# Last squares summed by TensorE, a fuller scan end, and later modulation in a two-block network

## The chip, the cores and the metric

The kernel runs on one core of one Trainium2 chip. The metric is device time of one execution in microseconds (us), as the median of three runs. TensorE is called PE in the rows, VectorE DVE, ScalarE ACT, GpSimd POOL and SyncE, which issues most transfers, SP.

## The reference, cut to what matters

Sequence 512, width 1024, batch 1, all in float32. A first block of two layers is followed by a second block of one even and one odd mixer and a final norm.

```python
def first_block(x, mem, positions, ...):
    h = x
    for l in range(2):
        hn = rms_norm(h, norm_mix_pre[l])
        proj = hn @ w_in[l]                     # split in 12 parts
        y_attn = dilated_attention_mixer(...)   # 256 wide
        y_conv = short_conv_mixer(...)          # 256 wide
        y_gdn = gated_deltanet_mixer(...)       # 512 wide; a scan over 8 chunks of 64
                                                # positions, then o = rms_norm(o, w) * gate
        mix = concatenate([y_attn, y_conv, y_gdn]) @ w_out[l]
        h = h + rms_norm(mix, norm_mix_post[l])
        hn = rms_norm(h, norm_xattn_pre[l])
        xa = memory_cross_attention(hn, rms_norm(mem, norm_mem[l]), w_xq[l], w_xkv[l], w_xo[l])
        h = h + rms_norm(xa, norm_xattn_post[l])
        hn = rms_norm(h, norm_ffn_pre[l])
        h = h + rms_norm(swiglu_ffn(hn, w_gate_up[l], w_down[l]), norm_ffn_post[l])
    return h

def second_block(x, c, ctx, c_ctx, mod_w, mod_b, norm_g, ...):
    for i in range(2):
        sh_l, sc_l, g_l = split(silu(c) @ mod_w[i] + mod_b[i], 3)      # the modulation
        sh_c, sc_c, g_c = split(silu(c_ctx) @ mod_w[i] + mod_b[i], 3)
        h_lat = rms_norm_2(x, norm_g[i]) * (1 + sc_l) + sh_l
        h_ctx = rms_norm_2(ctx, norm_g[i]) * (1 + sc_c) + sh_c
        y, y_ctx = (even_mixer if i == 0 else odd_mixer)(h_lat, h_ctx, ...)
        x = x + g_l * y                          # the odd mixer holds a 31-tap depthwise
        ctx = ctx + g_c * y_ctx                  # convolution beside its attention
    return rms_norm_2(x, final_g)
```

## The kernel before, in words

*Layout.* Everything is feature-major: the residual stream `hT` is 8 chunks of 128 features by 512 positions. A matrix product runs in three products of rounded float32 (`mm3`, lines 293 to 295): weight and input are each split in a high part (`wh`, `xh`) and a residual (`wl`, `xl`), and high x high, high x low and low x high are summed in PSUM. One output tile of 128 x 512 is 8 chunks x 3 = 24 matmuls. A weight tile arrives by DMA from SP's queue (`wr`, 3 buffers), is rounded on ACT (`wh`, line 266) and its residual taken on DVE (`wl`, line 267), 4 buffers each. PSUM has three kinds of tile, two of each: `g` and `b` of one bank, `s` of two.

*Statistics.* The RMS norms need a sum over features, that is over partitions. ACT squares each chunk (line 392), DVE adds the squares into `acc` (line 393), and TensorE multiplies `acc` with a matrix of ones in full float32 (line 378, in `rsqrt_of`); ACT makes R, the reciprocal root, from the sum with Ln and Exp. `residual_stat` (line 404) does so for each output chunk that TensorE leaves in PSUM, after copying it to `om`. `residual` (line 409) then scales `om` by R, adds it to `hT`, splits the new chunk into `xh` and `xl` for the next product, which is begun with each chunk (`begin`, `advance`), and `prestat` (line 429) takes the statistics of the new `hT` for the next norm. That R is applied when the product's tiles are evicted (line 454, `fg`). Such ends stand at mix_post, x_post and f_post of each layer.

*What sets the order.* Each engine runs its instructions in the order in which a scheduler set them at build time; priorities follow the order of the code. Where a chain leaves TensorE without work, the code interleaves other work by generators: `self.fill` is a list of them, `pump(n)` takes n steps from the first, `drain` takes all. The memory's and the context's projections, the gates and the short convolution are such fills. Rates say how many steps come with one piece of the main work: RATES[l] in the feed-forward part of layer l (layer 1's fill is the context stream, `ctx_stream`), CR in odd attention, where the fill is the 31-tap convolution on DVE (`conv31`, line 1777) and what surrounds it, spread over 32 items of attention.

*The scan's end.* `gdn_scan` (line 822) runs eight chunks in sequence. The last one's output goes to `O` (L855 is its last product), then `gdn_norm` (line 880) four times: ACT squares, DVE scales `O`, TensorE transposes it (line 888), DVE multiplies it into `om`. `mix_out` had begun tiles 0 and 1 of w_out with input chunks 0 to 3, which come from attention and convolution; behind the norms chunks 4 to 7 are split and `advance`d.

*The first block's end.* `residual` of f_post1 leaves the new `hT`; `colstat` (line 1355) squares its 8 chunks, adds 7 of them on DVE, sums on TensorE; `modnorm` (line 1335) makes `xh` and `xl` chunk by chunk with R and the modulation, and TensorE starts the even mixer's first product (`ev_in`). The context stream is pumped around it.

*The modulation* (`mod_dot`, line 1311) is 96 dot products of 1024 elements on DVE with weights from `mw`, a fill of layer 0's feed-forward part. They may not be issued before a named instruction: `last`, the last split of x_post0's residual.

Of the kernel before, what the change touches and what calls it, by code (L numbers as in the profile page):

```python
# [12 lines left out]
AF = mybir.ActivationFunctionType  # L13
# [4 lines left out]
D = 1024  # L18
S = 512
CTX = 256  # L20
MEM = 256
KC = D // 128
HID = 2816
HC = HID // 128
# [5 lines left out]
TS, TB = 2, 2  # L30
WP, XP = 1, 2
ER, OR = 1, (1.6, 2.1, 2.1, 1.7)
CR = 1.5
XOP = (0, 1)
RATES = (0.7, 1.1)
WR, WH, WL = 3, 4, 4
HA, HB, HD = 0, 0, 0
MP = (0, 0)
# [172 lines left out]
class Net:  # L211
# [128 lines left out]
    def begin(self, aps, extra=0):  # L340
# [7 lines left out]
        for i, ap in enumerate(aps):  # L348
            wh, wl = self.weight(ap)
            self.begun.append(((ap.tensor.name, ap.offset), wh, wl, ps[i]))  # L350

    def advance(self):
        c = self.nbegun
        self.nbegun += 1
        for _, wh, wl, ps in self.begun:
            self.mm3(ps, wh[:, c], wl[:, c], self.xh[:, c], self.xl[:, c], c == 0, c == KC - 1)


    def pump(self, n=1):
# [15 lines left out]
    def rsqrt_of(self, ss, out, scale, epscol, n=512, lhs=None):  # L375
        nc = self.nc
        ps = self.bps()[:, :n]
        nc.tensor.matmul(ps, self.ones if lhs is None else lhs, ss, start=True, stop=True)  # L378
        bias = 0.0 if epscol is None else self.epst[:, epscol:epscol + 1]
        nc.scalar.activation(out, ps, AF.Ln, bias=bias, scale=scale)  # L380
        nc.scalar.activation(out, out, AF.Exp, scale=-0.5)
        return ps

    def sumsq(self, acc, src, first, t=None):

        nc = self.nc
        if first:
            nc.scalar.activation(acc, src, AF.Square)
        else:
            if t is None:  # L390
                t = self.tmp("sq")[:, :acc.shape[-1]]
            nc.scalar.activation(t, src, AF.Square)  # L392
            nc.vector.tensor_add(acc, acc, t)  # L393

    def split(self, h, l, src, w=None):

# [5 lines left out]


    def residual_stat(self, c, ps, acc):
        nc = self.nc
        nc.scalar.copy(self.om[:, c], ps)
        self.sumsq(acc, ps, c == 0)

    def residual(self, acc, post, pre=None, R=None, scale=1.0 / D, epscol=0, chunk=2, aeps=0, keep=False):
        nc = self.nc  # L410
        Rp = self.R
        self.pump(2)
        with self.hp(HA):
            self.rsqrt_of(acc, Rp, 1.0 / D, aeps)
        self.pump(3)
        for c in range(KC):
            self.pump(chunk)
            t = self.tmp("rt")
            with self.hp(HB):
                nc.vector.scalar_tensor_tensor(t, self.om[:, c], self.sm(post, c), Rp, ALU.mult, ALU.mult)  # L420
                nc.vector.tensor_add(self.hT[:, c], self.hT[:, c], t)
                if pre is not None:
                    self.last = self.split(self.xh[:, c], self.xl[:, c], self.hT[:, c], self.sm(pre, c))
            if pre is not None:
                self.advance()
        if pre is not None:
            self.prestat(R, scale, epscol, keep)

    def prestat(self, R, scale=1.0 / D, epscol=0, keep=False):
        nc = self.nc  # L430
        acc = self.tmp("acc2", bufs=1)
        for c in range(KC):
            self.sumsq(acc, self.hT[:, c], c == 0)
        ps = self.rsqrt_of(acc, R, scale, epscol)
        if keep:

            self.zacc = self.tmp("acc", bufs=1)
            nc.scalar.activation(self.zacc, ps, AF.Identity, bias=self.epst[:, 3:4], scale=8.0 * EPS / D)
# [17 lines left out]
    def out_proj(self, w, pump=0):  # L456
        acc = self.tmp("acc", bufs=1)
        for c in range(KC):
            ps = self.gemm(w[c], (self.xh, self.xl))
            self.residual_stat(c, ps, acc)  # L460
            self.pump(pump)
        return acc

    def silu(self, out, x, t):

# [39 lines left out]
    def first(self, dbg=None):  # L505
# [5 lines left out]
        for l in range(2):  # L511
            self.mark(f"mix{l}")
            self.mixer(l)
            if dbg and dbg(self, f"mix{l}"): return
            self.mark(f"xattn{l}")
            self.xattn(l)
            if l == 0:
                with tc.tile_pool(name="md", bufs=1) as p:
                    self.mod_start(p)
                    csb = self.mod_rows(p)  # L520
                    dots = [self.mod_dot(i, p, csb, 0, 24) for i in range(2)]
                    acc = self.xo_ffn(l, dbg, 1, dots + [self.mod_end(0), self.mod_end(1)])
                    self.drain()
                    self.begin([w[1][c] for c in range(2)], 2)
                    self.residual(acc, "f_post0", "mix_pre1", self.R, chunk=1, aeps=None)
                if dbg and dbg(self, f"h3_{l}"): return
            else:
                self.ctxp = self.ctx.enter_context(tc.tile_pool(name="keep", bufs=1))
                self.Vc = self.ctxp.tile([128, 2, 2, 128], F32, name="vc")
                self.kd = [[self.dr.tile([128, CTX], F32, name=f"kd{i}{u}") for u in "hl"] for i in range(6)]  # L530
                self.dv = self.ctxp.tile([128, 2, 512], F32, name="dvc")
                with tc.tile_pool(name="ctx", bufs=1) as p:
                    self.fill = [self.ctx_stream(p)]
                    acc = self.xo_ffn(l, dbg, 1)
                    self.residual(acc, "f_post1", chunk=1, aeps=None)
                    if dbg and dbg(self, f"h3_{l}"): return
                    self.mark("ctxend")
                    R = self.colstat(self.hT, S, self.R)
                    self.pump(2)
                    self.begin([a["ev_in"][c] for c in (4, 0, 5)])  # L540
                    for _ in self.modnorm(0, 0, self.hT, self.xh, self.xl, S, R):
                        self.advance()
                        self.pump()
                    self.drain()
# [277 lines left out]
    def gdn_scan(self, l, p, heads):  # L822
# [3 lines left out]
        for c in range(8):  # L826
# [38 lines left out]
            if c == 7:  # L865
                while len(self.fill) > 3:
                    self.pump()
                for i in range(4):
                    self.gdn_norm(l, O, i, p)
        self.drain()  # L870
        self.mark(f"gdnend{l}")
        for h in range(4):
            self.split(self.xh[:, 4 + h], self.xl[:, 4 + h], self.om[:, 4 + h])
            self.advance()

    def gdn_norm(self, l, O, i, p):

# [330 lines left out]
    def ffn(self, l, rate):  # L1208
# [13 lines left out]
        w = max(PARTS[l])  # L1222
        ends = np.cumsum(PARTS[l]).tolist()
        parts = list(zip([0] + ends, ends))
        def down(ti, yh, yl):
            lo, hi = parts[ti]
            for c in range(KC):
                ps = self.gemm(a["w_down"][l][c][:, lo:hi], (yh, yl), k=hi - lo)
# [1 line left out]
                    nc.scalar.copy(self.om[:, c], ps)  # L1230
                else:
                    nc.vector.tensor_add(self.om[:, c], self.om[:, c], ps)  # L1232
                    if hi == HC:
                        self.sumsq(acc, self.om[:, c], False)
                step()

        with tc.tile_pool(name=f"ff{l}", bufs=2) as p:
# [73 lines left out]
    def mod_dot(self, i, p, csb, n0, n1):  # L1311

        nc, a = self.nc, self.a
        last = self.last[1].ins
        for n in range(n0, n1):
            raw = self.tmp("mw", (128, 2, 512), pool=p, bufs=2).rearrange("p a b -> p (a b)")
            nc.sync.dma_start(raw, a[f"mod_t{i}"][n - 4 * MP[i]])
# [531 lines left out]
```

## Time and profile before

| | |
|---|---|
| median of 3 runs | 2509.55 us (2506.88 to 2512.07) |
| profiled execution | 2508.96 us |
| its span | 2507.2 us |
| mean granted clock of TensorE | 0.986 |
| TensorE busy | 2409.2 us, 96% |
| VectorE busy | 1755.7 us, 70% |
| ScalarE busy | 1272.1 us, 51% |
| DMA | 263.30 MB, mean 105 GB/s |

All rows are of one profiled execution; times in them count from the start of its span. The busy time of TensorE is modelled from the ends of pipelined matmuls. A timeline row is: start, duration, engine, line, operation, output<-inputs, count, and in brackets how long the engine sat idle ahead of it and for what. A window row is: stretch, its length, then busy time and number of instructions of PE, weight loads (PEld), DVE, ACT and POOL, the granted clock (1.00 is full), the DMA engines' mean share and GB/s.

### The profile page before, as it was taken

What the parts mean: (1) busy time and instruction counts of PE and PEld (TensorE: products, weight loads), DVE (VectorE), ACT (ScalarE), POOL (GpSimd) and SP (SyncE); (2) the same over time, 40 slices, a digit from 0 to 9 for tenths busy, and PEclk for the clock granted to TensorE, in tenths of its full rate; (3) what the DMA queues carried; (4) which work ended last, traced back from release to release, by engine and by line L of the source; (5) the groups of instructions that cost most, each with busy time, mean ns of one, the idle gap of its engine ahead of it and who ended that gap; (6) DMA issues with size and microseconds to landing.
All of it is one profiled execution on the core that took longest, in us unless ns stands there. A gap on an engine that the chain in (4) does not pass through costs nothing.

```text
span 2507.2 us, 34818 instructions
## 1 busy us (share of the span) xinstructions
PE 2409.2 (96%) x13036; PEld 1960.1 (78%) x13036; DVE 1755.7 (70%) x3164; ACT 1272.1 (51%) x2371; POOL 22.6 (1%) x57
## 2 busy tenths in 40 slices
PE   8999899989999989998999999999998999999998
PEld 6678688768888766786887678888876888878787
DVE  7887675499984578876755755556566666669975
ACT  5754454444333447544545644445344666545584
POOL 0000000000000000000000000000000000000000
PEclk9999999999999999999999999999999999999999
DMA  5133133237753321331332233233335421333422
GB/s 180 51 86 77 51 118 126 93 115 238 214 174 109 97 83 51 86 77 51 125 120 78 83 97 97 93 100 127 118 116 155 119 64 56 115 101 99 115 77 68
DMA packets 96025, 263.30 MB, mean 105 GB/s; under 512 B 16232, under 2 KB 32232, under 8 KB 94704
## 3 DMA queue, kind: packets, MB, share of 16 engines
q1 hardware_dynamic: 92592, 257.72, 33.8%
q0 software_dynamic: 704, 2.17, 0.5%
q10 hardware_dynamic: 2560, 1.18, 0.3%
q8 instruction: 103, 1.69, 0.3%
q14 instruction: 66, 0.54, 0.1%
HBM read 240.83 MB, written 4.46 MB: 98 GB/s over the span
## 4 chain that ended last, share of the span: by engine, by line
PE 84%; DVE 9%; ACT 3%; DMA 2%; issue 2%; ACTq 0%; DVEq 0%; SPq 0%
PE g L293 19%; PE g L294 18%; PE g L295 18%; PE b L810 3%; PE s L293 3%; PE s L294 3%; PE s L295 3%; PE s L757 2%; PE b L1417 2%; PE b L378 2%; DVE wl L267 1%; DVE mj L1321 1%; PE b L797 1%; DMA mw<-in_mod_t_dram 1%; PE s L855 1%
## 5 line engine op out<-in xcount | busy, mean ns | idle before, releaser
L293 PE MATMUL g<-xh,wh 128*128 128x512 f32 (+1 forms) x1960 | 784.5, 402 | 40.1 <-ACT xh L400 9.1
L295 PE MATMUL g<-xh,wl 128*128 128x512 f32 (+1 forms) x1960 | 775.1, 396 | 6.0 <-DVE wl L267 5.9
L294 PE MATMUL g<-xl,wh 128*128 128x512 f32 (+1 forms) x1960 | 777.2, 397 | 0.0
L266 ACT CAST wh<-wr 128x1024 fp32r<-128x1024 f32 (+4 forms) x422 | 397.7, 945 | 632.5 <-PE g L294 492.7
L267 DVE TENSOR_TENSOR wl<-wr,wh 128x1024 fp32r<-128x1024 f32 (+4 forms) x422 | 458.4, 1089 | 162.6 <-ACT wh L266 156.5
L293 PEld LDWEIGHTS g<-xh,wh 128*128 128x128 f32 x1960 | 371.9, 190 | 128.1 <-ACT xh L400 12.1
L295 PEld LDWEIGHTS g<-xh,wl 128*128 128x128 f32 x1960 | 372.8, 190 | 85.5 <-DVE wl L267 8.0
L294 PEld LDWEIGHTS g<-xl,wh 128*128 128x128 f32 x1960 | 373.3, 190 | 76.0 <-issue 2.4
L293 PE MATMUL g<-yh,wh 128*128 128x512 f32 x352 | 139.8, 398 | 1.8 <-DVE om L1232 1.7
L294 PE MATMUL g<-yl,wh 128*128 128x512 f32 x352 | 138.1, 392 | 0.0
L295 PE MATMUL g<-yh,wl 128*128 128x512 f32 x352 | 137.9, 392 | 0.1
L1321 DVE CUSTOM_DVE_ANT_0 mj<-mw,csb 128x1024 f32<-128x1024 f32 x96 | 117.2, 1221 | 7.1 <-DMA mw<-in_mod_t_dram 6.0
L1232 DVE TENSOR_TENSOR om<-om,g 128x512 f32<-128x512 f32 x80 | 54.9, 686 | 63.6 <-PE g L295 63.2
L810 PE MATMUL b<-ident,P 128*128 128x128 f32 x608 | 96.0, 277 | 0.4 <-ACT P L783 0.3
L817 ACT COPY pt<-b 128x512 f32<-128x512 f32 (+3 forms) x136 | 71.6, 535 | 45.5 <-PE b L810 44.1
L468 ACT ACTIVATE rt<-rt 128x512 f32<-128x512 f32 x76 | 47.9, 631 | 91.6 <-DVE rt L467 90.5
L810 PEld LDWEIGHTS b<-ident,P 128*128 128x128 f32 x608 | 69.7, 141 | 24.0 <-ACT P L783 6.2
L454 DVE TENSOR_TENSOR fg<-g,R 128x512 f32<-128x512 f32 x42 | 29.0, 690 | 81.3 <-PE g L295 77.4
L783 ACT ACTIVATE P<-P,st 128x512 f32<-128x512 f32 (+4 forms) x96 | 65.9, 687 | 39.0 <-DVE st L779 16.7
L757 PE MATMUL s<-K,Q 128*128 128x256 f32 (+2 forms) x384 | 84.8, 338 | 0.0
L393 DVE TENSOR_TENSOR acc<-acc,sq 128x512 f32<-128x512 f32 (+1 forms) x111 | 75.6, 681 | 5.9 <-ACT sq L392 4.1
L293 PEld LDWEIGHTS g<-yh,wh 128*128 128x128 f32 x352 | 66.2, 188 | 17.1 <-issue 2.5
(444 smaller groups left out, 3899.8 us busy)
## 6 DMA issues: line engine op xcount, KB each, us to landing
wr<-in_w_gu_dram SPq DMA_DIRECT2D x88, 512.0 KB
wr<-in_w_in_dram SPq DMA_DIRECT2D x56, 512.0 KB
mw<-in_mod_t_dram SPq DMA_DIRECT2D x48, 512.0 KB
wr<-in_ev_in_dram SPq DMA_DIRECT2D x40, 512.0 KB
wr<-in_od_in_dram SPq DMA_DIRECT2D x32, 512.0 KB
wr<-in_w_down_dram SPq DMA_DIRECT2D x56, 192.0 KB
wr<-in_w_down_dram SPq DMA_DIRECT2D x24, 384.0 KB
wr<-in_w_out_dram SPq DMA_DIRECT2D x16, 512.0 KB
```

The source lines that it names most:

```text
L266: nc.scalar.copy(hi[:, :k], raw[:, :k])
L267: nc.vector.tensor_sub(lo[:, :k], raw[:, :k], hi[:, :k].bitcast(F32))
L293: mm(ps, wh, xh, start=first, stop=False)
L294: mm(ps, wh, xl, start=False, stop=False)
L295: mm(ps, wl, xh, start=False, stop=last)
L393: nc.vector.tensor_add(acc, acc, t)
L757: self.nc.tensor.matmul(sp[:, c], q, K[u][:, k:k + c.stop - c.start], start=u == 0, stop=u == 1)
L783: nc.scalar.activation(P[:, c], src[i], AF.Exp, bias=shift, scale=-1.0 if neg else 1.0, accum_out=one(3 + i))
L810: nc.tensor.transpose(ps[:, 128 * (j % 4):128 * (j % 4) + 128], P, self.ident)
L817: nc.scalar.copy(out(j - m + 1, m), src)
L1232: nc.vector.tensor_add(self.om[:, c], self.om[:, c], ps)
L1321: nc.vector.tensor_tensor_reduce(out=junk, in0=raw, in1=csb[:, b], scale=1.0, scalar=0.0, op0=ALU.mult, op1=ALU.add, accum_out=self.mod[i] ...
```

## The change

Six edits, made together:

- CR from 1.5 to 1.1 and RATES[1] from 1.1 to 1.07.
- Scan end: `begin_more` begins w_out tiles 2 and 3 in an `s` tile with input chunks 0 to 3, as a fill that runs before and during the norms; behind them only two `advance`s, now over four tiles, and `finish` for the rest.
- Last chunk of a residual's statistics (`residual_stat`, and `down` for f_post): its square is taken first and summed by TensorE on its own, as a second accumulating matmul behind the one of `acc`, instead of being added to `acc` by DVE. In `residual_stat` the copy to `om` follows the square. Six places: mix_post, x_post and f_post of both layers.
- First block's end (`stat=True`): each new `hT` chunk is squared and goes to an accumulating matmul with ones at once; `colstat` with its 7 adds goes, `rsqrt_end` takes the sum.
- `mod_dot`: the dots may be issued behind `prestat`'s last add instead of the last split.

```diff
 ER, OR = 1, (1.6, 2.1, 2.1, 1.7)
-CR = 1.5
+CR = 1.1
-RATES = (0.7, 1.1)
+RATES = (0.7, 1.07)
...
+    def begin_more(self, aps):
+        p = self.sps()
+        for i, ap in enumerate(aps):
+            wh, wl = self.weight(ap)
+            ps = p[:, 512 * i:512 * i + 512]
+            self.begun.append(((ap.tensor.name, ap.offset), wh, wl, ps))
+            for c in range(self.nbegun):
+                self.mm3(ps, wh[:, c], wl[:, c], self.xh[:, c], self.xl[:, c], c == 0, False)
+                if c % 2:
+                    yield
...
+    def finish(self):
+        for _, wh, wl, ps in self.begun:
+            for c in range(self.nbegun, KC):
+                self.mm3(ps, wh[:, c], wl[:, c], self.xh[:, c], self.xl[:, c], c == 0, c == KC - 1)
+        self.nbegun = KC
...
     def rsqrt_of(self, ss, out, scale, epscol, n=512, lhs=None):
-        nc.tensor.matmul(ps, self.ones if lhs is None else lhs, ss, start=True, stop=True)
+        ss = ss if isinstance(ss, list) else [ss]
+        for i, t in enumerate(ss):
+            nc.tensor.matmul(ps, self.ones if lhs is None else lhs, t, start=i == 0, stop=i == len(ss) - 1)
+        self.rsqrt_end(ps, out, scale, epscol)
+        return ps
...
     def residual_stat(self, c, ps, acc):
+        if c == KC - 1:
+            t = self.tmp("sq")
+            nc.scalar.activation(t, ps, AF.Square)
+            nc.scalar.copy(self.om[:, c], ps)
+            return [acc, t]
         nc.scalar.copy(self.om[:, c], ps)
         self.sumsq(acc, ps, c == 0)
...
+                if stat:
+                    sq = self.tmp("sq")
+                    nc.scalar.activation(sq, self.hT[:, c], AF.Square)
+                    if c == 0:
+                        ps = self.bps()
+                    nc.tensor.matmul(ps, self.ones, sq, start=c == 0, stop=c == KC - 1)
...
         for c in range(KC):
-            self.sumsq(acc, self.hT[:, c], c == 0)
+            self.added = self.sumsq(acc, self.hT[:, c], c == 0)
...
-                    self.residual(acc, "f_post1", chunk=1, aeps=None)
+                    ps = self.residual(acc, "f_post1", chunk=1, aeps=None, stat=True)
-                    R = self.colstat(self.hT, S, self.R)
+                    R = self.R
+                    self.rsqrt_end(ps, R, 1.0 / D, 0)
...
                 while len(self.fill) > 3:
                     self.pump()
+                self.fill.append(self.begin_more([a["w_out"][l][c] for c in (2, 3)]))
                 for i in range(4):
                     self.gdn_norm(l, O, i, p)
         self.drain()
         for h in range(4):
             self.split(self.xh[:, 4 + h], self.xl[:, 4 + h], self.om[:, 4 + h])
-            self.advance()
+            if h < 2:
+                self.advance()
+        self.finish()
...
-                    if hi == HC:
+                    if hi == HC and c < KC - 1:
                         self.sumsq(acc, self.om[:, c], False)
+                    elif hi == HC:
+                        sq = self.tmp("sq")
+                        nc.scalar.activation(sq, self.om[:, c], AF.Square)
+                        acc = [acc, sq]
...
     def mod_dot(self, i, p, csb, n0, n1):
-        last = self.last[1].ins
+        last = self.added.ins
```

How the instructions stand on the engines, at three places. A name's number counts tiles and differs between the two kernels; line numbers are each kernel's own.

TensorE at the end of layer 0's scan, before: the last product with `at`, the second and third group of transposes (`b<-ident,O`), then w_out tiles 0 and 1 (`g`) with the split scan output.

```order
L855 MATMUL s_2402<-vn_2403,at_1065 64x128
L888 MATMUL b_2493<-ident,O_2041 128x128 x4
L888 MATMUL b_2512<-ident,O_2041 128x128 x4
L293 MATMUL g_2418<-xh,wh_2422 128x512
L293 MATMUL g_2419<-xh,wh_2428 128x512
```

The same place with the change:

```order
L895 MATMUL s_2402<-vn_2403,at_1065 64x128
L294 MATMUL s_2545<-xl,wh_2548 128x512
L295 MATMUL s_2545<-xh,wl_2549 128x512
L293 MATMUL s_2545<-xh,wh_2548 128x512
L294 MATMUL s_2545<-xl,wh_2548 128x512
L295 MATMUL s_2545<-xh,wl_2549 128x512
L293 MATMUL s_2545<-xh,wh_2566 128x512
L294 MATMUL s_2545<-xl,wh_2566 128x512
L931 MATMUL b_2493<-ident,O_2041 128x128 x4
```

Between the last product and the second transposes stand seven matmuls of w_out tiles 2 and 3 (`s_2545`). Seven more stand ahead of the four `at` products, eight ahead of the third transposes and two behind these; 24 in all, which before stood behind the scan.

TensorE at the end of the first block, before: context products (lines 325 to 327), the one sum (L378), and the even mixer's first products.

```order
L326 MATMUL s_15725<-wl_15828,ch 128x512
L327 MATMUL s_15725<-wh_15827,cl 128x512
L378 MATMUL b_15821<-acc_1545_15798,ones 128x512
L293 MATMUL g_15844<-xh,wh_15849 128x512
L293 MATMUL g_15845<-xh,wh_15855 128x512
L293 MATMUL s_15846<-xh,wh_15861 128x512
```

With the change, where the sums of two `hT` chunks (L459) stand:

```order
L459 MATMUL b_15642<-sq_15764,ones 128x512
L325 MATMUL s_15748<-wh_15751,ch 128x512
L326 MATMUL s_15748<-wl_15752,ch 128x512
L327 MATMUL s_15748<-wh_15751,cl 128x512
L325 MATMUL s_15748<-wh_15751,ch 128x512
L326 MATMUL s_15748<-wl_15752,ch 128x512
L327 MATMUL s_15748<-wh_15751,cl 128x512
L459 MATMUL b_15642<-sq_15776,ones 128x512
L325 MATMUL s_15748<-wh_15781,ch 128x512
```

There are eight such sums, with 6 context matmuls of 512 columns or 10 to 12 of 256 between two of them and 14 behind the last. f_post1's own two sums stand behind 3 context matmuls, where there were 28.

VectorE in x_post0's `prestat`, before: the adds into `acc` and the modulation's dots (L1321).

```order
L393 TENSOR_TENSOR acc_415_4321<-acc_415_4321,sq_4326 128x512
L1321 ISA mj_4369,mod_80<-mw_4367,csb_3996 128x1024
L1321 ISA mod_80 128x1
L393 TENSOR_TENSOR acc_415_4321<-acc_415_4321,sq_4329 128x512
L1321 ISA mj_4369,mod_80<-mw_4367,csb_3996 128x1024
L1321 ISA mod_80 128x1
L393 TENSOR_TENSOR acc_415_4321<-acc_415_4321,sq_4332 128x512
```

With the change:

```order
L418 TENSOR_TENSOR acc_414_4320<-acc_414_4320,sq_4331 128x512
L267 TENSOR_TENSOR wl_4454<-wr_4451,wh_4453 128x1024
L418 TENSOR_TENSOR acc_414_4320<-acc_414_4320,sq_4334 128x512
L418 TENSOR_TENSOR acc_414_4320<-acc_414_4320,sq_4337 128x512
L267 TENSOR_TENSOR wl_4498<-wr_4495,wh_4497 128x1024
L418 TENSOR_TENSOR acc_414_4320<-acc_414_4320,sq_4340 128x512
L1370 ISA mj_4368,mod_80<-mw_4366,csb_3995 128x1024
```

The dots stand behind the last add; the sum for R stands 13 matmuls earlier on TensorE. In odd attention the convolution's taps end at item 23 of 32 where they ended at item 21, and 7 weight residuals stand ahead of item 16 where there were 4 or 5.

## Rows read from the trace of the kernel before

**Rows 1.** The page: busy time, share and instructions of each engine.
```profile
PE 2409.2 (96%) x13036; PEld 1960.1 (78%) x13036; DVE 1755.7 (70%) x3164; ACT 1272.1 (51%) x2371; POOL 22.6 (1%) x57
```
**Rows 2.** Waits of PE's queue: us in total, times, longest.
```profile
PE b L378 <- DVE acc L393: 16.1, 6, 4.7
```
**Rows 3.** Windows (columns as told above): a full stretch of layer 0's feed-forward.
```profile
600.00:640.00 40.00, 40.00 (x179) 33.10 (x178) 38.66 (x62) 17.22 (x24) 0.00 (x0) 1.00 0.69 204
```
**Rows 4.** Timeline of PE (columns as told above), end of layer 0's scan.
```profile
285.32 1.08 PE L855 MATMUL s<-vn,at 64*64 64x128 f32 x8 [1.24 <-ACT O L838]
...
287.93 0.88 PE L888 MATMUL b<-ident,O 128*128 128x128 f32 x4 [1.53 <-DVE O L885]
...
290.47 1.09 PE L888 MATMUL b<-ident,O 128*128 128x128 f32 x4 [1.66 <-DVE O L885]
...
293.17 0.80 PE L293 MATMUL g<-xh,wh 128*128 128x512 f32 x1 [1.62 <-ACT xh L399]
```
**Rows 5.** Windows at the scan's end, layer 0 and layer 1.
```profile
283.40:293.20 9.80, 3.75 (x24) 2.54 (x22) 6.25 (x16) 3.06 (x13) 0.00 (x0) 0.74 0.05 10
293.20:298.40 5.20, 5.20 (x12) 4.06 (x13) 3.30 (x6) 2.93 (x7) 0.00 (x0) 0.50 0.47 187
1169.30:1172.20 2.90, 2.90 (x7) 2.28 (x8) 2.45 (x4) 1.48 (x3) 0.00 (x0) 0.50 0.78 322
```
**Rows 6.** Timeline of ACT, DVE and PE, last chunk of x_post0's statistics.
```profile
499.86 0.58 ACT L406 COPY om<-g 128x512 f32<-128x512 f32 x1
500.34 0.60 ACT L392 ACTIVATE sq<-g 128x512 f32<-128x512 f32 x1
...
501.13 0.69 DVE L393 TENSOR_TENSOR acc<-acc,sq 128x512 f32<-128x512 f32 x1
...
501.87 0.70 PE L378 MATMUL b<-acc,ones 128*128 128x512 f32 x1 [2.77 <-DVE acc L393]
```
**Rows 7.** Timeline of ACT, DVE and PE, last chunk of f_post0's statistics.
```profile
876.77 0.63 ACT L392 ACTIVATE sq<-om 128x512 f32<-128x512 f32 x1
...
877.98 0.69 DVE L393 TENSOR_TENSOR acc<-acc,sq 128x512 f32<-128x512 f32 x1
...
878.72 2.07 PE L378 MATMUL b<-acc,ones 128*128 128x512 f32 x2 [2.76 <-DVE acc L393]
```
**Rows 8.** Windows behind x_post0's and f_post0's waits.
```profile
507.20:513.50 6.30, 6.26 (x14) 4.53 (x15) 6.30 (x11) 4.14 (x7) 0.00 (x0) 0.50 0.01 3
884.90:888.90 4.00, 3.96 (x9) 2.71 (x10) 4.00 (x7) 2.89 (x5) 0.00 (x0) 0.50 0.00 0
```
**Rows 9.** Timeline of PE, f_post1's sum between context matmuls.
```profile
1874.47 1.02 PE L378 MATMUL b<-acc,ones 128*128 128x512 f32 x2
...
1875.45 0.28 PE L294 MATMUL s<-cl,wh 128*128 128x256 f32 x1
```
**Rows 10.** The page's costliest groups: the modulation's dots.
```profile
L1321 DVE CUSTOM_DVE_ANT_0 mj<-mw,csb 128x1024 f32<-128x1024 f32 x96 | 117.2, 1221 | 7.1 <-DMA mw<-in_mod_t_dram 6.0
```
**Rows 11.** Timeline of PE, layer 0's feed-forward, behind the first eviction.
```profile
534.94 0.50 PE L293 MATMUL g<-xh,wh 128*128 128x512 f32 x1 [1.67 <-DVE fg L454]
```
**Rows 12.** Timeline of DVE, last `hT` chunk of the first block.
```profile
1891.72 1.28 DVE L421 TENSOR_TENSOR hT<-hT,rt 128x512 f32<-128x512 f32 x2
```
**Rows 13.** Timeline of PE, first block's end.
```profile
1902.30 1.74 PE L378 MATMUL b<-acc,ones 128*128 128x512 f32 x2 [4.71 <-DVE acc L393]
...
1907.02 1.22 PE L293 MATMUL g<-xh,wh 128*128 128x512 f32 x2 [2.98 <-ACT xh L1342]
```
**Rows 14.** Windows: from the last down matmul to the first ev_in matmul.
```profile
1868.40:1907.00 38.60, 26.45 (x148) 20.82 (x146) 32.97 (x44) 21.50 (x31) 0.00 (x0) 0.94 0.65 204
```
**Rows 15.** Windows: the first ev_in matmuls.
```profile
1907.00:1912.90 5.90, 5.88 (x14) 4.62 (x15) 5.65 (x9) 2.94 (x5) 0.00 (x0) 0.50 0.67 229
```
**Rows 16.** Timeline of PE, odd attention.
```profile
2356.25 0.50 PE L295 MATMUL g<-xh,wl 128*128 128x512 f32 x1 [4.12 <-DVE wl L267]
```
**Rows 17.** Windows: behind that wait.
```profile
2356.30:2360.10 3.80, 3.80 (x10) 2.98 (x11) 3.80 (x9) 1.94 (x5) 0.00 (x0) 0.55 0.37 138
```
**Rows 18.** Tile `cu`: the convolution's taps, duration in ns least/median/most.
```profile
L1795 DVE SCALAR_TENSOR_TENSOR om<-cu,small,om x90: 720/736/746, 2257.3 to 2378.9; 128x497 f32<-128x497 f32 x6, 128x498 f32<-128x498 f32 x6, 128x499 f32<-128x499 f32 x6, 128x500 f32<-128x500 f32 x6
```

More of the change, by code (lines that the diff above doesn't have):

```diff
@@ L377, in rsqrt_of, with rsqrt_end @@
         ps = self.bps()[:, :n]
-        nc.tensor.matmul(ps, self.ones if lhs is None else lhs, ss, start=True, stop=True)
+        ss = ss if isinstance(ss, list) else [ss]
[3 more added lines that the diff above has]
+        return ps
+    def rsqrt_end(self, ps, out, scale, epscol):
+        nc = self.nc
         bias = 0.0 if epscol is None else self.epst[:, epscol:epscol + 1]
@@ L381, in rsqrt_of @@
         nc.scalar.activation(out, out, AF.Exp, scale=-0.5)
-        return ps
     def sumsq(self, acc, src, first, t=None):
@@ L392, in sumsq @@
             nc.scalar.activation(t, src, AF.Square)
-            nc.vector.tensor_add(acc, acc, t)
+            return nc.vector.tensor_add(acc, acc, t)
     def split(self, h, l, src, w=None):
@@ L405, in residual_stat, with residual @@
         nc = self.nc
+        if c == KC - 1:
[3 more added lines that the diff above has]
+            return [acc, t]
         nc.scalar.copy(self.om[:, c], ps)
         self.sumsq(acc, ps, c == 0)
-    def residual(self, acc, post, pre=None, R=None, scale=1.0 / D, epscol=0, chunk=2, aeps=0, keep=False):
+    def residual(self, acc, post, pre=None, R=None, scale=1.0 / D, epscol=0, chunk=2, aeps=0, keep=False, stat=False):
         nc = self.nc
@@ L427, in residual @@
             self.prestat(R, scale, epscol, keep)
+        return ps if stat else None
     def prestat(self, R, scale=1.0 / D, epscol=0, keep=False):
@@ L459, in out_proj @@
             ps = self.gemm(w[c], (self.xh, self.xl))
-            self.residual_stat(c, ps, acc)
+            r = self.residual_stat(c, ps, acc)
             self.pump(pump)
-        return acc
+        return r
     def silu(self, out, x, t):
@@ L1225, in down @@
         def down(ti, yh, yl):
+            nonlocal acc
             lo, hi = parts[ti]
```

## The prediction

> **What bounds the kernel now.** I read the page's first part: TensorE (PE) is busy 2409.2 us of a 2507.2 us span, VectorE (DVE) 1755.7, ScalarE (ACT) 1272.1 [rows 1]. TensorE is the bound nearly everywhere, so an edit is worth what it takes out of TensorE's idle time, out of stretches in which TensorE runs at half its clock, or out of its instruction count. The remaining 98 us are the first two together in small pieces. Then the waits of TensorE's queue: the largest that this change touches is the one for the running sum of squares (DVE `acc`, 16.1 us in 6 waits) [rows 2]. Then the timeline at each such wait, and the windows around it for the clock. The price of a matmul of 512 columns at full clock comes from a window in which TensorE never idles: 179 in 40.00 us, 0.223 us each [rows 3]. Where the granted clock is 0.50 (1.2 instead of 2.4 GHz) I count the stretch less its matmuls at 0.223 as what the clock costs.
>
> **The change, part by part.**
>
> *Scan end, both layers.* At the end of layer 0's scan TensorE waits 1.24, 1.53, 1.66 and 1.62 us in turn, for the output chunk and the norms, and has nothing else queued [rows 4]; layer 1 shows the same four to 0.01 us. The change puts 24 ready matmuls there: 7 ahead of the waiting `at` products, 7 ahead of the second transposes, 8 ahead of the third, 2 behind. 7 x 0.223 = 1.56 and 8 x 0.223 = 1.78 fill the first three gaps (1.24 + 1.53 + 1.66), the last one gets 0.45: 4.88 a layer, 9.7 in all. The same 24 matmuls leave the stretch behind the gaps, so this is idle time removed and no work added. It needs the weights of w_out tiles 2 and 3 in time; their casts already stood in the scan, and move on no engine.
>
> The granted clock is 0.74 over those gaps and 0.50 right behind them, for 12 matmuls in 5.20 us in layer 0 and 7 in 2.90 us in layer 1 [rows 5]. At 0.223 they would take 2.68 and 1.56, so the fall costs 2.5 + 1.3 = 3.8. With the gaps mostly filled I expect TensorE to keep its clock: -3.8. If it does not, 0; both stay in the range.
>
> [...]
>
> *Last square.* In x_post0 ACT copies (0.58), then squares (0.60), DVE adds (0.69), and TensorE's sum starts at 501.87 after a wait of 2.77 [rows 6]. Now the square goes first, and the sum takes `acc` and the square in two accumulating matmuls. The first runs in the wait, the second does what the old one did. Of the path go the copy and the add, together 1.27: -1.3. f_post0 has no copy ahead of its square, but the add (0.69) goes and the 0.58 between the square's end (877.40) and the add's start: -1.3, and its sum took 2.07 because the clock had fallen in the 2.76 us wait [rows 7]; with half of that wait I take 1.0 back: -2.3. The half clock of 4.00 and 6.30 us behind these two [rows 8] stays in my sum, since a 4 us wait for the next `xh` is still there.
>
> From the start of an fp32 sum to that of the second context matmul behind it TensorE takes 0.98 us (1874.47 to 1875.45) [rows 9]; less 0.11 for one matmul of 256 columns, the sum costs 0.87. At the other three sites (mix_post twice, x_post1) matmuls of the memory or context stream already stand ahead of the sum, so nothing is waited for and the second sum is added work: 3 x 0.87 = +2.6. In x_post1 only 5 context matmuls stand ahead where there were 24; a wait of up to 1.3 is then paid back by an earlier R: 0, with 1.3 either way in the range.
>
> *Modulation behind R.* 96 dots of 1.221 us each [rows 10] stood between the adds of x_post0's statistics, so R came late and the first `fg` made TensorE wait 1.67 us [rows 11]. Now the adds come first: -1.7. What is late next is the dots themselves; their results are read only in the second block, and DVE has the whole feed-forward part for them. If the dots pile up before weight residuals there, that is lost again: 0 is the other end.
>
> *First block's end.* Before, the last hT chunk lands at 1893.0 [rows 12]; then come the squares and adds of all eight, a sum that waits 4.71, and a first ev_in matmul that waits 2.98 and starts at 1907.02 [rows 13]. Now each chunk's square goes to its own sum. By the chain: 1893.0, 0.63 for the square, some 0.25 in handing over, then the old path from the sum to the first `xh` (1907.02 - 1902.30 = 4.72): 1898.6, 8.4 earlier. By TensorE's work: it was busy 26.45 of the 38.60 us from 1868.4 to 1907.0 [rows 14]. Eight more fp32 sums (7 of the chunks, 1 of f_post1) add 7.0, and the last one at full clock saves 0.9, so with no idle at all it would need 32.5, 6.1 less. f_post1's own sum now stands behind 3 context matmuls instead of 28, so TensorE waits there for add and square, about 0.69 + 0.6 = 1.2. I take 6.1 - 1.2 = -4.9. The far end: only the two waits, 4.71 + 2.98 = 7.7, go against 7.0 of sums: -0.7. Behind it 14 matmuls ran in 5.90 us at 0.50 [rows 15], 2.8 more than at full clock; with both waits gone: -2.8. Together -7.7.
>
> *Rates.* TensorE waits 4.12 us for a weight residual `wl` at 2356.25 in odd attention [rows 16], and then runs at 0.55: 10 matmuls in 3.80 us, 1.6 over 2.23 [rows 17]. With CR 1.1 a conv tap (0.736 us [rows 18]) comes every 0.91 items instead of 0.67, and the residuals reach DVE earlier: 7 by item 16, where there were 4 or 5. Up to -5.7; DVE has as much to do, so the wait may shift; I take -4.0. Far end: a wait elsewhere as long as this one, 0 to +5. RATES[1] moves context steps by 3% in a stretch where TensorE is full: 0.
>
> **Sum.** -9.7 - 3.8 - 1.3 - 2.3 - 1.7 - 7.7 - 4.0 + 2.6 = -27.9. The profiled execution took 2508.96 (span 2507.2): 2481.1. It is 0.6 below the median of 2509.55, which makes 2481.7. I give 2482.
>
> **Rivals.**
>
> *A. Clock and block end give little.* TensorE's gaps become shorter, but the granted clock falls all the same, and the block end gives only its far end. Then -9.7 - 1.3 - 1.3 - 1.7 - 0.7 - 2 + 2.6 = -14.1: 2495. For it: in x_post0 and f_post0 one wait of about 4 us remains in any case. Against it: the scan's gaps fill to three quarters.
>
> *B. The new rate makes a new wait.* With CR 1.1 the last taps are at item 23 of 32 instead of 21, and the convolution's norm stands in TensorE's queue behind them. Were 15 taps late there, at 0.736, that is 11 us; with the 4.0 not gained, -27.9 + 15 = -13: 2497. Against it: nine items still lie behind the last tap.
>
> *C. Slower: sums block TensorE's queue.* Each of the block end's 8 sums needs a chunk that DVE and ACT have just made. If each waits 1 us with the context matmuls behind it, and the last-square sums stall 2.8 each at x_post1 and f_post1, that is 13.6, and all 13 new sums on the path add 11.3; against gains of only 9.7 + 1.7: +13.5, 2523. It decides once a chunk takes longer than the 6 to 12 context matmuls between two sums (1.3 us). For it: DVE's two operations on a chunk alone take 1.28 [rows 12], and weight residuals come between. Against it: TensorE was idle 12.15 us in that stretch, and that pays for the waits.
>
> The Trainium skill, PSUM — Partial Sum Buffer, section Engine vs sequencer instructions, says that matmuls start and complete in program order. That is the condition of rival C: nothing passes a waiting sum. The rows agree where a sum waits (4.71 with nothing in it), though whether context matmuls were ready then they do not show.
>
> **How the numbers follow.** Forecast 0.62, A 0.22, B 0.11, C 0.05. The forecast's own range is 2472 to 2490: low, if x_post0's and f_post0's half clock goes too (6.30 - 14 x 0.223 = 3.2, and 2.0) and the odd part gives all 5.7; high, if the clock terms (6.6) and 2 of the odd part fail. Over the cases the range is 2469 to 2499, which leaves C and the worst of B outside. A measurement of this kernel tells 0.2% (5 us) from no change. Faster by more 0.92 (the forecast, A, B but for a tail), within 0.03 + 0.02 = 0.05 (tails of A and B), slower 0.03 (part of C).
>
> **What the profile after would show.** Scan: matmuls of `s` between the transposes, no idle over 0.7 us, granted clock 1.00 behind. Last square: two sums in a row, the first with no wait of its own, the second about 1.3 us sooner. Block end: first ev_in matmul 5 us sooner after the last down matmul, at full clock. Dots: first `fg` wait gone. Odd: no wait over 2 us for `wl` and none for the convolution's norm. Wrong would be: a wait for a square over 1.5 us before each of the block end's sums (C), or 0.50 behind the scan (A).

## The result and the profile after

The changed kernel takes 2476.4 us (median of 4 runs, 2473.16 to 2477.97), the kernel before 2509.54 (2506.88 to 2512.07): ratio 0.9866, 95% interval 0.9849 to 0.9883, which is -33.1 us. The forecast was 2482, -27.9.

The profiled execution after took 2473.16 (span 2471.4), the fastest of its four, and 35.8 less than the profiled one before. Some 2.7 of that stand ahead of anything that the change touches: its first matmul starts at 7.19 us instead of 9.08, a half-clock stretch near 161 us lasts 3.41 us instead of 6.83, and at the last state update of layer 0's scan it is 2.7 ahead. This part is spread between executions: over the traces of all versions that place lies between 2.8 us ahead of the kernel before and 0.7 behind it. To see where the rest came from, I read the start of the same instruction in both traces at twelve places; the step between two places is what the stretch gained.

| from ... to | ahead at its end, us | step, us | forecast, us |
|---|---|---|---|
| start, to layer 0's scan, last state update | 2.7 | -2.7 | 0 |
| scan end, mix_post, memory attention 0 | 10.8 | -8.0 | -6.5 |
| x_post0, to the first down product | 14.0 | -3.2 | -3.0 |
| feed-forward 0 | 12.8 | +1.2 | 0 |
| f_post0, mixer 1, to the scan's last state update | 14.3 | -1.5 | -2.3 |
| scan end, mix_post, memory attention 1 | 21.05 | -6.75 | -5.3 |
| x_post1, to the first down product | 20.15 | +0.9 | +0.9 |
| feed-forward 1 | 24.1 | -3.9 | 0 |
| first block's end, to the even mixer's first scores | 32.1 | -8.0 | -7.7 |
| even mixer, odd mixer's beginning | 30.75 | +1.35 | 0 |
| odd attention | 36.3 | -5.6 | -4.0 |
| odd mixer's and final end | 35.8 | +0.5 | 0 |

The page's first part: TensorE idles 65.6 us of its span (2471.4 - 2405.8) where it idled 98.0, and is busy 3.4 us less (2409.2 in [rows 1]) though 13 sums were added. The clock records go with that: the granted clock is 0.50 for 74.0 us in nine stretches before, and for 35.2 us in six after.

```profile
PE 2405.8 (97%) x13062; PEld 1957.3 (79%) x13062; DVE 1746.9 (71%) x3151; ACT 1269.9 (51%) x2371; POOL 22.5 (1%) x57
```

*Scan end.* The timeline of TensorE at the end of layer 0's scan answers to [rows 4], and the windows to [rows 5].

```profile
282.91 1.08 PE L895 MATMUL s<-vn,at 64*64 64x128 f32 x8
285.67 0.60 PE L931 MATMUL b<-ident,O 128*128 128x128 f32 x4
287.95 0.60 PE L931 MATMUL b<-ident,O 128*128 128x128 f32 x4
290.17 0.74 PE L293 MATMUL g<-xh,wh 128*128 128x512 f32 x2 [1.15 <-ACT xh L424]
```
```profile
281.00:288.60 7.60, 7.60 (x43) 5.99 (x42) 5.30 (x14) 2.37 (x11) 0.00 (x0) 1.00 0.00 1
288.60:294.00 5.40, 4.25 (x19) 3.08 (x18) 3.37 (x6) 2.36 (x5) 0.00 (x0) 1.00 0.58 197
1154.90:1158.00 3.10, 3.07 (x13) 2.45 (x14) 2.50 (x4) 1.54 (x3) 0.00 (x0) 1.00 0.76 307
```

Of the four waits (6.05 us) only the last is left, 1.15 us, and the granted clock is 1.00 behind both scans, where it was 0.50.

*Last square.* TensorE at x_post0 (answers to [rows 6]) and at f_post0 ([rows 7]), then the windows behind them ([rows 8]).

```profile
488.20 1.02 PE L399 MATMUL b<-acc,ones 128*128 128x512 f32 x2
489.76 1.13 PE L399 MATMUL b<-sq,ones 128*128 128x512 f32 x2 [0.54 <-ACT sq L434]
495.14 1.22 PE L293 MATMUL g<-xh,wh 128*128 128x512 f32 x2 [4.25 <-ACT xh L425]
...
863.00 1.02 PE L399 MATMUL b<-acc,ones 128*128 128x512 f32 x2
864.66 1.13 PE L399 MATMUL b<-sq,ones 128*128 128x512 f32 x2 [0.64 <-ACT sq L1282]
869.94 0.80 PE L293 MATMUL g<-xh,wh 128*128 128x512 f32 x1 [4.16 <-ACT xh L425]
```
```profile
495.10:500.00 4.90, 4.86 (x12) 3.45 (x13) 4.90 (x8) 2.89 (x5) 0.00 (x0) 0.56 0.01 3
869.90:874.90 5.00, 4.96 (x11) 3.52 (x12) 5.00 (x9) 2.89 (x5) 0.00 (x0) 0.51 0.00 0
```

The first sum finds its input ready, the second waits 0.5 to 0.6 us for the square. It starts 1.79 and 1.90 us behind the last matmul of the product, where the one sum before started 3.16 behind it at both places: 1.37 and 1.26 sooner. The wait for the next `xh` stays (4.25 us in x_post0 in both traces, 4.15 and 4.16 in f_post0), and half clock still goes with it, for 6.83 us at each place where it was 10.24.

*First block's end*, the timeline of TensorE (answers to [rows 13]) and the window of the first ev_in matmuls ([rows 15]).

```profile
1846.38 1.10 PE L399 MATMUL b<-acc,ones 128*128 128x512 f32 x2 [0.98 <-DVE acc L418]
...
1867.40 1.02 PE L459 MATMUL b<-sq,ones 128*128 128x512 f32 x2
1869.64 1.02 PE L459 MATMUL b<-sq,ones 128*128 128x512 f32 x2
1873.81 0.72 PE L293 MATMUL g<-xh,wh 128*128 128x512 f32 x2
```
```profile
1873.80:1880.00 6.20, 6.20 (x28) 5.10 (x28) 6.20 (x9) 2.89 (x4) 0.00 (x0) 1.00 0.45 158
```

The first line is f_post1's own sum. None of the eight sums of a chunk waits, and no ev_in matmul does: the 14 context matmuls behind the last sum keep TensorE busy while ACT and DVE make the reciprocal root and the first split. The clock stays at 1.00.

### The profile page after: what moved, and what is told of

It reads as the page before. It is cut to its first block, busy times and chain, and to the rows that moved or that the text cites. A ratio compares the mean times of both kernels' runs of the same rounds, so it can differ in the third digit from the quotient of the medians.

```text
span 2471.4 us, 34861 instructions
## 1 busy us (share of the span) xinstructions
PE 2405.8 (97%) x13062; PEld 1957.3 (79%) x13062; DVE 1746.9 (71%) x3151; ACT 1269.9 (51%) x2371; POOL 22.5 (1%) x57
## 3 DMA queue, kind: packets, MB, share of 16 engines
q10 hardware_dynamic: 2560, 1.18, 0.3%
q8 instruction: 103, 1.69, 0.3%
## 4 chain that ended last, share of the span: by engine, by line
PE 83%; DVE 9%; ACT 3%; DMA 2%; issue 2%; SPq 0%; ACTq 0%; DVEq 0%
PE g L293 18%; PE g L294 17%; PE g L295 17%; PE s L293 3%; PE s L295 3%; PE s L294 3%; PE b L850 3%; PE s L797 2%; PE b L1466 2%; PE b L399 2%; DVE wl L267 1%; DVE mj L1370 1%; PE b L837 1%; DMA mw<-in_mod_t_dram 1%; ACT wh L266 1%
## 5 line engine op out<-in xcount | busy, mean ns | idle before, releaser
L293 PE MATMUL g<-xh,wh 128*128 128x512 f32 (+1 forms) x1928 | 767.4, 400 | 32.8 <-ACT xh L425 8.4
L294 PE MATMUL g<-xl,wh 128*128 128x512 f32 (+1 forms) x1928 | 760.8, 395 | 1.1 <-DVE xl L426 0.7
L295 PE MATMUL g<-xh,wl 128*128 128x512 f32 (+1 forms) x1928 | 758.1, 393 | 1.9 <-DVE wl L267 1.8
L293 PEld LDWEIGHTS g<-xh,wh 128*128 128x128 f32 x1928 | 363.6, 189 | 117.3 <-ACT xh L425 10.2
L295 PEld LDWEIGHTS g<-xh,wl 128*128 128x128 f32 x1928 | 364.2, 189 | 78.4 <-DVE wl L267 3.8
L294 PEld LDWEIGHTS g<-xl,wh 128*128 128x128 f32 x1928 | 364.8, 189 | 75.1 <-DVE xl L426 2.5
L295 PEld LDWEIGHTS g<-yh,wl 128*128 128x128 f32 x352 | 66.1, 188 | 15.1
```

Source lines behind the costliest of these rows:

```text
L293: mm(ps, wh, xh, start=first, stop=False)
L294: mm(ps, wh, xl, start=False, stop=False)
L295: mm(ps, wl, xh, start=False, stop=last)
```

## The experiments

Twelve versions were timed beside the kernel before, with four to eleven executions of each. The ratio is to that kernel, and the interval beside it is the 95% one; times of a trace are of one profiled execution each.

### Each edit alone

**Scan end.** `begin_more`, `finish` and the two `advance`s, nothing else.

> The kernel before with the scan-end edit alone (w_out tiles 2 and 3 begun ahead of the norms). Forecast: the three waits of 1.2 to 1.7 us go in both layers and the half clock behind them too: -9.7 - 3.8 = -13.5 us, granted clock 1.00 behind both scans. Rival A (the clock falls all the same): -9.7 us, granted clock 0.50 for some 5 and 3 us behind the scans. If the profile of the full change is read right (its layer 0 came 8.0 us and its layer 1 6.8 us sooner over this end and mix_post, which lost two extra sums), this alone gives -15 to -17.

2494.49 against 2509.14, 0.9937 (0.9923 to 0.9951): -14.7. The window over the last transposes and the last wait:

```profile
285.50:291.00 5.50, 4.35 (x24) 3.11 (x22) 3.19 (x7) 2.60 (x10) 0.00 (x0) 1.00 0.23 66
```

Granted 1.00: the clock term holds in this trace, and A falls here. The two scan ends gave 8.9 and 7.6 in it. The traced execution is the fastest of five: two took 2489.3 and 2489.9 at a mean granted clock of 0.990, three 2494.5 to 2495.0 at 0.986 to 0.988. Where those three lost clock no trace shows.

**Last square.** `rsqrt_of` with a list, `residual_stat` and `down`.

> The last-square edit alone, six sites. Forecast: x_post0 -1.3, f_post0 -2.3, three covered sums +2.6, f_post1 near 0: -1 us; the second sum's wait 0.5 to 0.7 us in x_post0 and f_post0. Rival A (no clock back): 0. Rival C (sums hold up the context matmuls at x_post1 and f_post1, 2.8 each): +4 to +6.

2502.6, 0.9974 (0.9964 to 0.9983): -6.5, beyond the -1 that I forecast, and C is excluded. By the same places in its trace: mix_post +0.9 and +1.1, x_post1 +0.8 (the second sum, as forecast), x_post0 -0.75, f_post0 -3.2 and, unforeseen, -3.4 from f_post1 to the even mixer. At f_post1 the sum starts 8.6 us before where it stood ([rows 9]; 3.0 of that was gained earlier on), behind few context matmuls, and almost without waiting:

```profile
1865.89 1.10 PE L380 MATMUL b<-acc,ones 128*128 128x512 f32 x2 [0.18 <-DVE acc L399]
1867.12 1.12 PE L380 MATMUL b<-sq,ones 128*128 128x512 f32 x2
```

So the residual starts sooner, and the context matmuls that had stood ahead of the sum are left to fill waits further on: those listed from there to the first ev_in matmuls add to 9.0 us, where they were 12.1.

**First block's end.** `stat=True` and `rsqrt_end`.

> The end of the first block alone: each new chunk's square straight to its own sum. Forecast: -7.7 us less what f_post1's second sum had cost in it, so -7 to -9, first ev_in matmul at full clock and no wait over 1 us ahead of any of the eight sums. Rival A: -0.7 and half clock there. Rival C: each sum waits about 1 us, +3 to +8.

2501.04, 0.9969 (0.9959 to 0.9979): -8.1. The first sum of a chunk waits, the others don't; C falls.

```profile
1885.51 1.12 PE L433 MATMUL b<-sq,ones 128*128 128x512 f32 x2 [0.89 <-ACT sq L430]
1887.19 1.02 PE L433 MATMUL b<-sq,ones 128*128 128x512 f32 x2
1889.43 1.02 PE L433 MATMUL b<-sq,ones 128*128 128x512 f32 x2
...
1904.73 0.74 PE L293 MATMUL g<-xh,wh 128*128 128x512 f32 x2 [0.31 <-ACT xh L1356]
```

The first ev_in matmul, the last line, comes 4.9 us sooner after the last down product than before, the forecast's own figure, and the matmuls behind it run at full clock. In the full change it comes 9.1 sooner, but only 8.0 are left at the even mixer's first scores.

**Dots.** The line that counts; `added` is the last add of `prestat`, as in the change.

```diff
-        last = self.last[1].ins
+        last = self.added.ins
```

> The dots behind the statistics of x_post0 alone. Forecast: the 1.67 us wait for the first eviction goes, -1.7 us. Rival (dots pile up before weight residuals later in the feed-forward part): 0, with a new wait of 1 to 2 us for a weight residual or an output there.

2509.34, 1.0001 (0.9992 to 1.001): +0.2, the rival's number; -1.7 lies just inside the interval, so the trace has to decide. What TensorE waited for from x_post0 to f_post0, first before, then with this edit (us in total, times, longest):

```profile
PE g L293 <- DVE fg L454: 1.7, 1, 1.7
PE g L293 <- DVE rt L1248: 0.6, 1, 0.6
```
```profile
PE g L293 <- DVE rt L1248: 1.8, 3, 1.0
```

The first eviction no longer waits, but TensorE waits 1.2 us more for the gated products `rt`: the same dots stand in DVE's queue a little later. Six of them ran ahead of the first `fg`, and six more between it and the third `rt`; with the edit it is two and eight. The third `rt`, with the dot ahead of it on DVE and TensorE's wait:

```profile
549.73 1.22 DVE L1321 CUSTOM_DVE_ANT_0 mj<-mw,csb 128x1024 f32<-128x1024 f32 x1
...
550.87 0.69 DVE L1248 TENSOR_TENSOR rt<-g,fg 128x512 f32<-128x512 f32 x1
...
551.70 0.47 PE L293 MATMUL g<-xh,wh 128*128 128x512 f32 x1 [1.04 <-DVE rt L1248]
```

In the trace the first down product comes 1.0 sooner, measured from the memory attention, and the last one only 0.4.

**CR 1.1.**

> CR 1.1 alone. Forecast: the 4.12 us wait for a weight residual in odd attention goes and the half clock behind it, nothing takes its place: -4.0 to -5.7 us. Rival B (the convolution's norm is late at the end of odd attention): a wait of up to 11 us there, 0 to +7.

2503.28 against 2509.57, 0.9977 (0.9967 to 0.9987): -6.3. In odd attention no wait of TensorE is listed any more, neither for `wl` nor for the convolution's norm: B falls.

**RATES[1] 1.07.**

> RATES[1] 1.07 alone: 0 within 2 us, since TensorE is full where the context steps run. If it matters, it is by what is left of the context stream to cover the end of the first block: 3% fewer steps are spent ahead of it, so the two weight waits there (1.39 and 1.26 us) and part of the 4.71 us wait would shrink, -1 to -4.

2503.8, 0.9975 (0.9966 to 0.9985): -5.8, against my 0. Windows from the first to the last down product of layer 1, before and with this edit:

```profile
1418.11:1867.74 449.63, 446.67 (x2364) 368.59 (x2362) 254.36 (x438) 211.60 (x404) 0.00 (x0) 1.00 0.34 106
```
```profile
1418.16:1864.12 445.96, 444.35 (x2363) 368.72 (x2362) 251.93 (x432) 209.60 (x400) 0.00 (x0) 1.00 0.34 107
```

The work is the same, 2364 and 2363 matmul records, but it takes 3.7 less. One wait of 1.18 us for `om` near the end is gone:

```profile
1859.83 0.47 PE L293 MATMUL g<-yh,wh 128*128 128x512 f32 x1 [1.18 <-DVE om L1232]
```

It is there, 1.18 to 1.22 us long, in the traces of all eight versions with 1.1 and in none of the six with 1.07. The other 2.5 are spread over the stretch, some between main products and some where a fill's small products meet them; which of them go, and why, I did not separate. Another 1.2 came at the block end.

### Do the parts add, and what holds them?

The six medians add to -41.1, the change gives -33.1. Two edits were taken out of the full change. The full change itself was not run beside these versions. I compare with its 2476.4, and also by the distance from the kernel before, whose median beside these versions was 2508.14 and beside the full change 2509.54; that moves each difference by 1.4.

> The changed kernel without the last-square edit. If the parts add, it loses the 6.5 us that this edit gave alone: 2483. If f_post1's earlier sum and the other edits at the block end take the same idle time, it loses about 3: 2479.

Full change without the last square: 2477.98 (0.9878, 0.9862 to 0.9895), 1.6 more than the full change (3.0 by the distance from the kernel before), not 6.5.

> The changed kernel with RATES[1] back at 1.1. If the parts add, it loses the 5.8 us of that edit alone: 2482. If only its gain within layer 1's feed-forward part is its own (3.7 there in the profile) and the rest is shared with the block end: 2480. Forecast of the prediction: 2476.

With RATES[1] at 1.1: 2479.36 (0.9888, 0.9871 to 0.9904), 3.0 more (4.4 by the distance from the kernel before), not 5.8; the 1.18 us wait for `om` is back. The intervals reach about 4 us to either side, so the two differences are rough: both point to less than the sum, but 5.8 is not excluded. The traces show where about half of the missing 8 us are. Three edits spend the same idle time at the block end, where [rows 14] show 12.15 us: from the last down matmul to the even mixer's first scores the eight sums alone gave 7.5, f_post1's earlier sum 3.4 and RATES 1.2, together 12.1, and the full change gave 8.0. The other half was not found.

> The changed kernel with the rest of the context stream taken ahead of f_post1's residual, so that no context matmul stands between the eight sums; the work is the same. If cover is what makes the sums free (forecast, and the condition of rival C), TensorE waits 1 to 2 us ahead of each sum, 10 to 16 in all, with 3 to 5 for the two reciprocal roots, and its clock falls there: 2476 + 15 to 25, so about 2491 to 2501, 0.993 to 0.997 of the kernel before. If sums in TensorE's queue cost only their own 0.87, it stays at 2476 (0.987).

```diff
+                    self.drain()
                     ps = self.residual(acc, "f_post1", chunk=1, aeps=None, stat=True)
```

2482.01 (0.9897, 0.9881 to 0.9914): 5.6 over the full change (7.0 by the distance from the kernel before), between the two numbers expected. The scheduler still let context matmuls in between the first sums, so the edit took only the last of the cover away. The last six sums and the first ev_in matmul:

```profile
1874.22 2.92 PE L459 MATMUL b<-sq,ones 128*128 128x512 f32 x6
1878.21 2.97 PE L459 MATMUL b<-sq,ones 128*128 128x512 f32 x6 [1.08 <-ACT sq L456]
...
1884.16 0.74 PE L293 MATMUL g<-xh,wh 128*128 128x512 f32 x2 [2.98 <-ACT xh L1392]
```

The 2.98 of [rows 13] are back to the last digit, with 1.08 ahead of a sum, and 3.41 us at half clock follow from 1885.45. The matmuls behind and between the last sums thus hide 4.06 us of waits, and a half clock. From the last down matmul to the even mixer's first scores this version takes 78.4 us, the full change 70.9 and the kernel before 79.0: without this cover nearly all of the block end's gain is gone. The price of a block end with no cover at all stays open.

### What does the clock ask for?

The scan-end edit alone, with one tile instead of two:

```diff
-self.begin_more([a["w_out"][l][c] for c in (2, 3)])
+self.begin_more([a["w_out"][l][c] for c in (2,)])
```

> The scan-end edit with one tile instead of two: w_out tile 2 alone is begun ahead of the norms, 12 matmuls a layer, 2.7 us at full clock, against 6.05 us of waits. If the clock follows the idle time gradually, half of the 3.8 us comes back and the kernel gains 2 x 2.7 + 1.9 = 7.3. If the clock falls as before, 5.4 and granted 0.50 behind the scans. If the first gaps decide, 5.4 + 3.8 = 9.2 and granted 1.00.

2501.62 (0.9963, 0.995 to 0.9975): -8.0, but at half clock. By time alone this is nearest to the gradual case (7.3), so the windows have to decide. With 12 matmuls the first two waits are filled and the last two are as before; the windows are those behind the scans of layer 0 and 1:

```profile
291.13 0.63 PE L911 MATMUL b<-ident,O 128*128 128x128 f32 x4 [1.66 <-DVE O L908]
293.38 1.22 PE L293 MATMUL g<-xh,wh 128*128 128x512 f32 x2 [1.62 <-ACT xh L419]
```
```profile
292.20:298.90 6.70, 5.52 (x13) 4.36 (x14) 3.57 (x8) 3.45 (x8) 0.00 (x0) 0.50 0.46 157
1166.00:1169.30 3.30, 3.30 (x9) 2.62 (x8) 1.79 (x4) 1.45 (x4) 0.00 (x0) 0.50 0.39 164
```

Two idle pieces of 1.66 and 1.62 us close together still cost the clock; the single 1.15 of the full edit does not. The stretch at half clock is shorter here, 10.2 us in both layers together where it was 17.1, which would give the gain beyond 5.4; but such lengths differ between executions too.

### A version that goes on

The last-square form at two more places, ahead of the odd mixer (shown) and in the final norm:

```diff
-        for c in range(KC):
+        for c in range(KC - 1):
             self.sumsq(acc, src[:, c], c == 0)
...
+        self.nc.scalar.activation(t, src[:, KC - 1], AF.Square)
...
-        self.rsqrt_of(acc, R, 1.0 / D, 0, n)
+        self.rsqrt_of([acc, t], R, 1.0 / D, 0, n)
```

> The changed kernel with the last-square form at two more places: the statistics ahead of the odd mixer (where TensorE waits 2.86 us for the last add) and both halves of the final norm (1.86 us). DVE's add and its hand-over go from both paths: -1 at the first, -0.6 to -1.2 at the last, 2474. If the half clock ahead of the odd mixer goes too, 2472; if the second sum's 0.87 at half clock stands on the path, 2476.

2473.48 (0.9866, 0.9846 to 0.9885). TensorE ahead of the odd mixer, in the change and in this version:

```profile
2176.76 1.10 PE L399 MATMUL b<-acc,ones 128*128 128x512 f32 x2 [2.86 <-DVE acc L418]
2180.84 1.22 PE L293 MATMUL g<-xh,wh 128*128 128x512 f32 x2 [2.98 <-ACT xh L1391]
```
```profile
2174.30 1.02 PE L399 MATMUL b<-acc,ones 128*128 128x512 f32 x2
2176.03 1.13 PE L399 MATMUL b<-sq,ones 128*128 128x512 f32 x2 [0.71 <-ACT sq L1410]
2180.14 1.22 PE L293 MATMUL g<-xh,wh 128*128 128x512 f32 x2 [2.98 <-ACT xh L1392]
```

The wait of 2.86 us is down to 0.71, as in x_post0. The version's median is 2.9 below the full change's, but each beside its own runs of the kernel before gives the same ratio, 0.9866. So it is faster than the kernel before, and a gain over the change is not shown.

> The version with the last-square form at eight places, with the dots back ahead of the statistics (behind the last split, as before). If the dots' move gives nothing in the whole either, it stays at 2473 to 2474 us: the wait for the first eviction (1.7 us) is back, and the waits for the gated product later in the feed-forward part shrink from 2.1 to below 1. If the prediction's -1.7 holds there, 2475.

2473.38 (0.986, 0.9844 to 0.9877): nothing is seen of the dots' place in the whole either. In its trace the 1.7 us wait for `fg` is back and the waits for `rt` are down to 0.6.

## Why the prediction was right, and where its steps were off

- *TensorE is the bound, and its idle time, its clock and its count are the price list.* Right: the gains that were traced to a cause lie in one of them, and the second sum at the three sites where other matmuls stand ahead of it cost +0.9, +1.1 and +0.8 (+2.6 forecast).
- *The sum of the terms.* Partly luck. The parts are worth more alone than forecast (-41.1 against -27.9), and together they give 8 us less than alone, which the prediction, adding its terms, did not allow for; the two errors cancel in part. The low end's own terms (5.2 and 1.7 below 2482) reach 2475 and not 2472; the measured time lies above both.
- *Scan end*: mechanism right, size low. 9.7 + 3.8 forecast, 16.5 in the trace of the edit alone, -14.7 by medians. The step that was short is the filling by 24 x 0.223, which took only the listed idle time. The start-to-start times show more: from the matmul ahead to the one behind, beyond the usual spacing, the four waits (listed as 1.24, 1.53, 1.66 and 1.62) lost 1.40, 1.69, 1.97 and 1.93 us, and one more behind the split (listed as 0.49, at 301.83) lost 0.66: 7.65 in all. With the edit 1.32 is left, so 6.3 a layer and not 4.9. Each wait thus cost 0.16 us more than its listed idle time at full clock and 0.31 at half clock, where the usual spacing is itself longer; why, the rows do not show. The sign "no idle over 0.7 us" failed: 1.15 was left, as the prediction's own filling (1.17 left) had said.
- *Clock behind the scans*: right, 1.00 in both. The advice of the Trainium skill on idle gaps (TensorE: Matmul & The Clock Gate, Why this matters for your kernels) speaks of single gaps longer than any of these, and does not cover two of 1.66 and 1.62 us close together, behind which the clock fell here; behind one of 1.15 it did not.
- *Last square*: right at x_post0 and f_post0, where the sum came 1.37 and 1.26 sooner (1.3 forecast for each). Off at f_post1, whose earlier sum I priced inside the block end as a loss of 1.2 (the wait is 0.98 in the full change) and which gains 3.4 alone. In the full change the whole edit is worth some 1.6 to 3.0, within about 4 us to either side; that this lies near the forecast of 1 says little.
- *Dots*: wrong. -1.7 was forecast, +0.2 measured alone and 0.1 between the last two versions. The failed step is "DVE has the whole feed-forward part for them": the dots run early in it and stand ahead of the gated products. I had named 0 as the other end of the term, but by weight residuals.
- *Block end*: right alone: -7.7 forecast, -8.1 by medians, 7.5 in its trace, sum waits under 1 us, and the 4.9 and the clock each come out. That the full change also shows -8.0 there is partly luck, since f_post1's sum and RATES, which the forecast did not count there, share in it. (The 1.28 us of [rows 12] that rival C takes for DVE's two operations on a chunk are two adds on two chunks.)
- *CR*: right, at the upper end or just beyond it (-5.6 in the trace, -6.3 alone; -4.0 taken, -5.7 allowed).
- *RATES[1]*: wrong, 0 forecast. "TensorE is full" did not hold: it idled 3.0 us in that stretch (449.63 less 446.67), 1.18 of it in one wait that a view of all waits would have shown. Why a lower rate takes that wait away stays open.

The two wrong terms (+1.7 and -3.9) and the low scan term (-3.0) add to the -5.2 between forecast and result, as read in single traces; the odd mixer's -1.6 and the even mixer's +1.35 nearly cancel. The latter, in code that the change leaves alone, also showed in two single edits (+1.0 and +1.5), and its cause stays open. Rival A fell by the clock rows behind the scans and the block end, B by the odd attention without waits, C by eight sums that wait less than 1 us each.

## What to carry to other kernels

Price a wait of a pipelined engine by the distance from start to start, not by its idle time, and add the half clock behind it. A chain's end can be shortened by letting the matrix engine sum what a slower engine added, as long as ready matmuls stand between the sums and behind the last one. Edits that fill the same idle stretch don't add, and work that is only released later on a busy engine makes someone else late.

## What the runs showed of the hardware that I had not expected

- The half-clock stretch behind the same wait differs between executions: behind layer 1's scan, with the same four waits, it was 6.83 us before (1165.40 to 1172.23) and 10.24 with the block end's edit alone (1161.65 to 1171.89). Near 161 us, in code that no edit touches, it was 6.83 in eight of the fourteen traces, 3.41 in the full change and absent with the scan's edit alone. Near 2.4 us waits in x_post1 it appeared in some versions (3.41 us in the full change, from 1383.43) and not before, where the wait was 2.38. At half clock matmuls of 512 columns stand 0.43 us apart (in the trace with half of the scan's fill, from 294.83), at full clock 0.23, so 3.41 us of it cost up to 1.6, by this estimate. The times of one kernel go with this: of 54 executions of the kernel before, 21 at a mean granted clock of 0.984 have a median of 2509.8 us, and 12 at 0.986 one of 2507.3.
- The granted clock fell behind two idle pieces of 1.66 and 1.62 us with matmuls of 0.63 between them, and stayed at 1.00 behind one of 1.15.
